# A hybrid decoder step on one core: casts pinned behind evictions, the key and value projection after the query, a norm statistic in another PSUM ring

## The chip, the cores and the metric

The kernel runs on one core of a Trainium2 chip. The metric is the device time of one execution in microseconds. A core has five engines with an in-order queue each: TensorE (PE in the profile, with its weight loads as PEld), VectorE (DVE), ScalarE (ACT), GpSimd (POOL) and SyncE (SP, which here only issues DMAs). ACT and POOL issue DMAs too.

## The reference

```python
h = _rmsnorm(x, n1)
z = h @ w_in
hq, hf, hi, hg, sq, sk, sv, ga, gb = jnp.split(z, np.cumsum(IN_SPLITS)[:-1], axis=-1)
...
m = jax.nn.sigmoid(ga) * y_a + jax.nn.sigmoid(gb) * y_b
x = x + m @ w_o
h2 = _rmsnorm(x, n2)
x = x + jnp.square(jax.nn.relu(h2 @ w_ff1)) @ w_ff2
return x, nk, nv, s_new.astype(x.dtype)
```

One layer, with d_model 1024 and d_ff 4096, is computed for a prompt of 2048 tokens and for 8 sequences of 4 new tokens; `y_a` is a gated recurrence (HGRN2), `y_b` attention over a window of 128 keys with sinks, and a last rmsnorm stands behind the layer. Everything is float32.

## The kernel before

**Precision.** Every float32 operand is kept as two parts in a format that TensorE takes: `hi`, a cast by ACT, and `lo`, the rest, a subtraction on DVE behind it (`split_out` L254 and L255 from a raw tile, `split_in` L148 and L149 in place). A product is then three matmuls, hi·hi, hi·lo and lo·hi (L262 to L264, and L1544 to L1546).

**Stages.** The prompt is worked on in four blocks of 512 tokens; two blocks, with the 32 sample tokens added to the second pair, are one superblock (sb 0 and sb 1). Each large product is done by Strassen's scheme with seven products of half matrices. Three kinds of them matter here:

- `z` (from block 2 on): h @ w_in for all of superblock 1, units `z1_n`. Ahead of it, block 2 projects key and value (`skv`, evicted by `st_skv`, L823) and query (`sq`, `st_sq`, L826) into four tiles `stage` of which each goes out by one DMA to `zqk` (L827, issued by ACT). `late_at(...)` runs, between chunks of these projections, what block 1 has left over: `n2.stat`, `n2.spread` and `h2_out` (L1369, eight POOL stores of the normalised rows `x_b` to `h2d`). The operand `zS3` takes the SBUF slot of `x_b`.
- `f0` and `f1`: the up projection w_ff1 with the squared relu, 16 units per superblock. Unit i does `a` (fB with w1B11, fC with w1B21), `b` (T2, T1, T3) and `c` (T4, B22). The first 6 or 10 units' `a` runs ahead; `Wpair.early` loads and casts their weights. `f1_fin` (L1455 to L1471) forms the sums that the next product needs and POOL stores them in `u_A11` to `u_S4` in DRAM.
- `f2_0` and `f2_1`: the down projection w_ff2 in steps (L1544 to L1546). Step 0 multiplies A12 with the weight block B21. Its groups g = 0 to 3 need an activation tile `f2A12g` (loaded in two halves by `u_load`, L1538) and two weight tiles `rw2B21_<sb><g><h>` (`w2_blk`, L1522); each load is followed by its cast on ACT and its subtraction on DVE. Group 3's second half holds rows that the last unit of f0 (f1) stores (`u_A12_3`).

**Order.** A scheduler lays out the instructions of each engine ahead of time, from its own estimates of when they can run; what is wrapped in `tc.keep_in_program_order` keeps its place in the program on its engine. Tiles come from pools with a fixed number of buffers: the weights from 12 tiles of `wtile`, PSUM from four rings of two banks (`tp`, `hg`, `sw`, `mm`). An instruction that needs a buffer waits in its engine's queue until its last user is done, and what stands behind it there waits too. The statistic of a norm (`stat`, L205) transposes the squares into a bank of a ring (L213, tile `n_fb`) and reduces them on DVE (L214). `n2.ring` names that ring; for the last block it is `hg`, which fC uses too.

## Time and profile before

| | us |
|---|---|
| median of 3 runs | 2850.28 |
| lowest, highest | 2846.7, 2858.54 |
| the profiled execution | 2848.76 |
| its span | 2847.0 |
| PE busy in it | 2744.2 (96%) |
| DVE busy | 1783.7 (63%) |
| ACT busy | 1112.4 (39%) |
| POOL busy | 490.9 (17%) |

The span is the time from the first to the last instruction of the profiled execution; its own time is 1.8 us longer. PE is busy for 96% of it, so what a change to the order can give or take lies in PE's idle time, and that is read from the waits of PE, place by place.

### The profile page before, as it was taken

To read this page: it belongs to the slowest core of one execution; us is meant where nothing else is said; L and a number is where in the kernel's file an instruction comes from. 1 tells how busy PE (TensorE), PEld (TensorE's weight loads), DVE (VectorE), ACT (ScalarE), POOL (GpSimd) and SP (SyncE) were. 2 spreads that over 40 slices of the span, in tenths; PEclk is the share of its full clock that TensorE was granted. 3 is DMA by queue.
4 is the path that set the end of the run, shared out by engine and by line. 5 is a ranking of instruction groups with operands and counts; after the bars stand their busy time and mean duration, and the time that the engine had idled before them with its cause. 6 is when DMAs were issued, how large, how long until landed. Compare 5 with 4: busy or idle time off the path is not lost.

```text
span 2847.0 us, 50088 instructions
## 1 busy us (share of the span) xinstructions
PE 2744.2 (96%) x20053; PEld 2412.9 (85%) x20053; DVE 1783.7 (63%) x2889; ACT 1112.4 (39%) x2070; POOL 490.9 (17%) x782
## 2 busy tenths in 40 slices
PE   8999999999999998999899999999998999999998
PEld 7788887888899967778798888787888999999998
DVE  5675646646765376436666777766567776664546
ACT  4542435323444343324334333424344233343342
POOL 1101211012200102320121122120003333320001
PEclk9999999999999999999999999999999999999999
DMA  5237652377633425541455444686556444485553
GB/s 190 73 113 238 209 180 74 110 244 255 229 127 107 148 88 188 173 136 53 127 171 188 164 159 157 223 307 246 203 182 220 152 148 153 143 292 183 186 188 122
DMA packets 344482, 487.60 MB, mean 171 GB/s; under 512 B 23433, under 2 KB 220825, under 8 KB 344249
## 3 DMA queue, kind: packets, MB, share of 16 engines
q1 hardware_dynamic: 289112, 329.10, 36.6%
q0 software_dynamic: 42880, 140.22, 13.5%
q10 hardware_dynamic: 12256, 15.08, 1.5%
q8 instruction: 157, 2.57, 0.4%
q14 instruction: 77, 0.62, 0.1%
HBM read 353.64 MB, written 130.68 MB: 170 GB/s over the span
## 4 chain that ended last, share of the span: by engine, by line
PE 66%; issue 13%; DMA 7%; DVE 6%; POOL 4%; ACT 3%; POOLq 0%; SPq 0%; ACTq 0%; DVEq 0%
PE f L1544 6%; PE f L1545 6%; PE f L1546 6%; PE fB_f L262 2%; PE fB_f L264 2%; PE fB_f L263 2%; PE fB_z L262 1%; PE fB_z L264 1%; PE fB_z L263 1%; PE wob L1353 1%; PE wob L1354 1%; PE wob L1352 1%; POOL u_S L1471 1%; DMA S<-dS 1%; PE ps_hfb L677 1%
## 5 line engine op out<-in xcount | busy, mean ns | idle before, releaser
L1544 PE MATMUL f<-f2S,hw2T 128*128 128x264 f32 (+1 forms) x576 | 183.9, 319 | 1.8 <-ACT hw2T L148 1.8
L1546 PE MATMUL f<-f2S,lw2T 128*128 128x264 f32 (+1 forms) x576 | 183.7, 319 | 1.6 <-DVE lw2T L149 1.6
L1545 PE MATMUL f<-f2S,hw2T 128*128 128x264 f32 (+1 forms) x576 | 183.5, 319 | 0.0
L262 PE MATMUL fB_f<-S,w1T_f 128*128 128x264 f32 (+1 forms) x384 | 123.1, 321 | 2.5 <-ACT c_f L325 1.7
L1544 PE MATMUL f<-f2A,h_w2B 128*128 128x264 f32 (+1 forms) x384 | 122.4, 319 | 0.0
L1545 PE MATMUL f<-f2A,h_w2B 128*128 128x264 f32 (+1 forms) x384 | 122.3, 319 | 0.0
L1546 PE MATMUL f<-f2A,l_w2B 128*128 128x264 f32 (+1 forms) x384 | 122.3, 318 | 0.0
L263 PE MATMUL fB_f<-S,w1T_f 128*128 128x264 f32 (+1 forms) x384 | 122.3, 319 | 0.0
L264 PE MATMUL fB_f<-S,w1T_f 128*128 128x264 f32 (+1 forms) x384 | 122.1, 320 | 0.0
L149 DVE TENSOR_TENSOR lw2T<-lw2T,hw2T 128x1024 fp32r<-128x1024 f32 x64 | 78.2, 1223 | 66.6 <-ACT hw2T L148 65.7
L148 ACT CAST hw2T<-lw2T 128x1024 fp32r<-128x1024 f32 x64 | 67.2, 1050 | 130.8 <-DMA lw2T<-w_T 130.7
L1352 PE MATMUL wob<-m_b,h_wob 128*128 128x512 f32 (+2 forms) x320 | 114.1, 357 | 3.1 <-ACT m_b L254 3.1
L1544 PEld LDWEIGHTS f<-f2S,hw2T 128*128 128x128 f32 x576 | 108.4, 188 | 10.0 <-ACT hw2T L148 2.7
L1546 PEld LDWEIGHTS f<-f2S,lw2T 128*128 128x128 f32 x576 | 108.0, 188 | 10.0 <-DVE lw2T L149 2.5
L1354 PE MATMUL wob<-m_b,l_wob 128*128 128x512 f32 (+2 forms) x320 | 113.3, 354 | 2.8 <-DVE l_wob L255 2.8
L1353 PE MATMUL wob<-m_b,h_wob 128*128 128x512 f32 (+2 forms) x320 | 113.7, 355 | 1.2 <-DVE m_b L255 1.1
L1545 PEld LDWEIGHTS f<-f2S,hw2T 128*128 128x128 f32 x576 | 108.4, 188 | 7.4
L149 DVE TENSOR_TENSOR f2S<-f2S 128x1024 fp32r<-128x1024 f32 (+1 forms) x64 | 79.0, 1240 | 43.7 <-ACT f2S L148 42.9
L254 ACT CAST w1T_f<-w1r_f 128x512 fp32r<-128x512 f32 x128 | 77.1, 619 | 72.7 <-DVE w1r_f L298 38.4
L255 DVE TENSOR_TENSOR w1T_f<-w1r_f,w1T_f 128x512 fp32r<-128x512 f32 x128 | 87.2, 688 | 26.8 <-ACT w1T_f L254 26.4
L1471 POOL DMA_DIRECT2D u_A<-c_f x106 | 57.3, 541 | 235.8 <-DVE c_f L1455 222.6
L1471 POOL DMA_DIRECT2D u_S<-s_f x144 | 77.7, 540 | 110.9 <-DVE s_f L1466 90.6
(843 smaller groups left out, 9277.2 us busy)
## 6 DMA issues: line engine op xcount, KB each, us to landing
w1r_f<-w_ff SPq DMA_DIRECT2D x64, 512.0 KB
lw2T<-w_T SPq DMA_DIRECT2D x64, 512.0 KB
rw2B<-w_ff SPq DMA_DIRECT2D x48, 512.0 KB
f2S<-u_S SPq DMA_DIRECT2D x32, 528.0 KB
ws<-w_ff SPq DMA_DIRECT2D x32, 512.0 KB
...
```

The source lines that it names most:

```text
L149: nc.vector.tensor_tensor(lo, F(lo), F(hi), ALU.subtract)
L255: nc.vector.tensor_tensor(dl, src, F(dh), ALU.subtract)
L262: nc.tensor.matmul(ps, wh, ah, start=(first and k == 0), stop=False, skip_group_check=not first)
L263: nc.tensor.matmul(ps, wh, al, start=False, stop=False, skip_group_check=not first)
L264: nc.tensor.matmul(ps, wl, ah, start=False, stop=(last and k == 3), skip_group_check=not first)
L1352: nc.tensor.matmul(p, wh, ah, start=(k == 0), stop=False)
L1353: nc.tensor.matmul(p, wh, al, start=False, stop=False)
L1354: nc.tensor.matmul(p, wl, ah, start=False, stop=(k == KD - 1))
L1471: nc.gpsimd.dma_start(us[o][u.n // 4][u.n % 4 * P:(u.n % 4 + 1) * P, u.t0:u.t0 + u.ln], y_)
L1544: nc.tensor.matmul(ps, wh, ah, start=first, stop=False, skip_group_check=cont)
L1545: nc.tensor.matmul(ps, wh, al, start=False, stop=False, skip_group_check=cont)
L1546: nc.tensor.matmul(ps, wl, ah, start=False, stop=lastk, skip_group_check=cont)
```

## The change

It does four things, and no instruction is added or taken away.

1. In block 2 the query is projected first and key and value second. The DMA to `zqk` moves from `st_sq` to `st_skv` with it, and the hooks of `late_at` move: the statistic and the spread run in the query's chunks 0 and 2, `h2_out` in the key and value's.
2. `split_in`, `split_out`, `Wpair.done` and `Wpair.early` get a switch that pins the cast and the subtraction in program order. `strassen_T` sets it for the first pair of each large product (z, f0, f1).
3. `w2_blk` and `u_load` move ahead of the pool of f1's tiles, and a new `begin()` loads and splits group 0 of f2's step 0, pinned; `strassen_T` calls it as `end`, after the last unit's `b` and ahead of its `c`.
4. The last block's `n2.ring` is `sw` and no longer `hg`.

```diff
--- before.py
+++ after.py
@@ -144,9 +144,12 @@
         split_out(wh, wl, raw)
         return wh, wl
 
-    def split_in(hi, lo):
-        nc.scalar.copy(hi, F(lo))
-        nc.vector.tensor_tensor(lo, F(lo), F(hi), ALU.subtract)
+    def pin(x, on=True):
+        return tc.keep_in_program_order(x) if on else x
+
+    def split_in(hi, lo, on=False):
+        pin(nc.scalar.copy(hi, F(lo)), on)
+        pin(nc.vector.tensor_tensor(lo, F(lo), F(hi), ALU.subtract), on)
 
     def unit_rows(w, k0, a, c0, nc_, name):
         src = w[k0 * P:(k0 + a) * P, c0:c0 + nc_].rearrange("(k p) c -> p k c", p=P)
@@ -250,10 +253,9 @@
         def scale(u, k, x):
             nc.vector.scalar_tensor_tensor(x, x, u.w[:, k:k + 1], u.acc, ALU.mult, ALU.mult)
 
-    def split_out(dh, dl, src):
-        nc.scalar.copy(dh, src)
-        nc.vector.tensor_tensor(dl, src, F(dh), ALU.subtract)
-
+    def split_out(dh, dl, src, on=False):
+        pin(nc.scalar.copy(dh, src), on)
+        pin(nc.vector.tensor_tensor(dl, src, F(dh), ALU.subtract), on)
 
     def prod(ps, wv, av, k0, t0, n, first, last=True):
         for k in range(4):
@@ -271,16 +273,16 @@
         def __init__(u, N, n, src, wt):
             u.N, u.n, u.src, u.wt, u.ops = f"{N}_{n}", n, src, wt, {}
 
-        def done(u, name, raw):
+        def done(u, name, raw, on=False):
             v = (u.wt if name in ("T3", "T4") else wtile)(F32R, f"w1{name}_{u.N}").rearrange("p (s k c) -> p s k c", s=2, k=4)
-            split_out(v[:, 0], v[:, 1], raw)
+            split_out(v[:, 0], v[:, 1], raw, on)
             u.ops[name] = v
 
-        def early(u):
+        def early(u, on=False):
             v = wtile(F32, f"w1r0_{u.N}").rearrange("p (s k c) -> p s k c", s=2, k=4)
             for kh in range(2):
                 nc.sync.dma_start(v[:, kh], u.src(u.n, kh)[:, 0:P].rearrange("(k p) c -> p k c", p=P))
-                u.done(f"B{kh + 1}1", v[:, kh])
+                u.done(f"B{kh + 1}1", v[:, kh], on)
 
         def rest(u):
             b = []
@@ -370,7 +372,7 @@
             tt(u.c12, u.pD, u.c12, ALU.add)
             u.fin(u, "c12", u.c12)
 
-    def strassen_T(N, npairs, src, chunks, A, st, fin, ahead, early, mid, free, wt):
+    def strassen_T(N, npairs, src, chunks, A, st, fin, ahead, early, mid, free, wt, end=None):
         ws = [Wpair(N, n, src, wt) for n in range(npairs)]
         nch = len(chunks)
         units = [Unit(i, ws[i // nch], *chunks[i % nch], A, st, fin) for i in range(npairs * nch)]
@@ -378,7 +380,7 @@
             units[-1].free, units[-1].ring = True, mm_ps
         for i in range(ahead):
             if i % nch == 0:
-                units[i].pair.early()
+                units[i].pair.early(i == 0)
             units[i].a(i < 4)
             early(i, units[i])
         for i, u in enumerate(units):
@@ -393,6 +395,8 @@
             u.b()
             if i == 0:
                 mid(u)
+        if end is not None:
+            end()
         units[-1].c()
 
     def chunks_of(n):
@@ -821,13 +825,13 @@
 
             def st_skv(ps, kind, c, nr):
                 nc.scalar.copy(stage[c][:, 512:768], ps)
+                nc.scalar.dma_start(zqk[sb][c * P:(c + 1) * P, :], stage[c])
 
             def st_sq(ps, kind, c, nr):
                 nc.scalar.activation(qk_out(stage[c][:, 0:512]), qk_in(ps), AF.Copy, scale=HD ** -0.5)
-                nc.scalar.dma_start(zqk[sb][c * P:(c + 1) * P, :], stage[c])
-
+
+            colN512(C_SQ, f"sq{B}", st_sq, late_at(0, 2))
             colN(C_SQ + 512, f"skv{B}", st_skv, late_at(1))
-            colN512(C_SQ, f"sq{B}", st_sq, late_at(0, 1))
             Th = Ths[sb]
             r0, r1 = z_half
             A = {"A11": hT_cur[0], "A12": hT_cur[1], "S1": opT(sb, 2, "zS1"), "S2": opT(sb, 3, "zS2"), "S3": opT(sb, 6, "zS3")}
@@ -1369,7 +1373,7 @@
                 nc.gpsimd.dma_start(h2d[sb][k * P:(k + 1) * P, z0:z0 + T], x1[:, k])
 
         if last_b:
-            n2.ring = hg_ps
+            n2.ring = sw_ps
         late += [n2.stat, n2.spread] + ([] if last_b else [h2_out])
     wk_ctx.close()
     cm_ctx.close()
@@ -1419,6 +1423,47 @@
         KG = NP // 4
         OPS = ("A11", "A12", "A22", "S1", "S2", "S3", "S4")
         us = {o: [tc.dram_tile([4 * P, Th], F32, name=f"u_{o}_{g}_{sb}") for g in range(KG)] for o in OPS}
+
+        slots = iter([0, 1] + [2, 3, 4, 5] * 8)
+        def w2_blk(o, k0, nk, c0, nc_, name, on=False):
+            r0, cs = k0 * P, slice(c0, c0 + nc_)
+
...
+            N = f"w2{o}_{name}"
+            if o[0] == "T":
+                wh, wl = wtile(F32R, "h" + N), wtile(F32R, "l" + N)
+                load(o, F(wl))
+                split_in(wh, wl, on)
+                return v3(wh), v3(wl)
+            x = wtile(F32, "r" + N)
+            load(o, x)
+            wh, wl = wtile(F32R, "h_" + N), wtile(F32R, "l_" + N)
+            split_out(wh, wl, x, on)
+            return v3(wh), v3(wl)
+
+        def u_load(o, g, on=False):
+            av = opv(next(slots), f"f2{o}{g}")
+            for k in range(0, 4, 2):
+                nc.sync.dma_start(lo_(av)[:, k:k + 2], us[o][g][k * P:(k + 2) * P, :].rearrange("(k p) t -> p k t", p=P))
+                split_in(av[:, 0, k:k + 2], av[:, 1, k:k + 2], on)
+            return av
+
+        begun = {}
+
+        def begin():
+            ao, wo = steps[0]
+            begun[ao] = u_load(ao, 0, True)
+            begun[wo] = [w2_blk(wo, 2 * h, 2, 0, 512, f"{sb}0{h}", True) for h in range(2)]
 
         with tc.tile_pool(name=f"f1_{sb}", bufs=1, reuse_waits="tile") as fp:
             def get(nm, slot):
@@ -1473,7 +1518,7 @@
             strassen_T(f"f{sb}", NP, lambda n, kh: w1[kh * 4 * P:(kh + 1) * 4 * P, 2 * n * P:2 * (n + 1) * P],
                        chunks, ff_ops,
                        lambda ln, name: fp.tile([P, ln], F32, tag="st", bufs=12 * len(chunks), name=name),
-                       f1_fin, 6 if len(chunks) == 1 else 10, early, mid, True, lambda dt, name: fp.tile([P, 1024], dt, tag="we", bufs=2, name=name))
+                       f1_fin, 6 if len(chunks) == 1 else 10, early, mid, True, lambda dt, name: fp.tile([P, 1024], dt, tag="we", bufs=2, name=name), begin)
 
         last = sb == nsb - 1
         fresh = (True, True, False, True, True, False, True)
@@ -1485,7 +1530,6 @@
         else:
             rings = ((tp_ps, hg_ps, mm_ps, sw_ps),) * 6 + ((hg_ps, mm_ps, sw_ps, hg_ps),)
         last = sb == nsb - 1
-        slots = iter([0, 1] + [2, 3, 4, 5] * 8)
         with tc.tile_pool(name=f"f2_{sb}", bufs=1, reuse_waits="tile") as fp:
             if last:
                 y1, xo = None, raw8(6, Th, f"xo{sb}")
@@ -1506,38 +1550,6 @@
                     return xo[:, regs[r], t0:t0 + ln]
 
                 return Fin(off[sb] + o * Th + t0, ln, lambda j: yacc[o][j][:, t0:t0 + ln], x, f2_ns, q)
-
-            def w2_blk(o, k0, nk, c0, nc_, name):
...
-            def u_load(o, g):
...
 
             def gemm2(ps, wh, wl, av, t0, ln, k, first, lastk, cont=False):
                 ah, al = av[:, 0, k, t0:t0 + ln], av[:, 1, k, t0:t0 + ln]
@@ -1571,8 +1583,9 @@
                     todo = [lambda: f0.sq(4, 5), lambda: f0.sq(6, 7), none, f0.stat, none, none, f0.spread] + [lambda j=j: f0.out(j) for j in range(KD)]
                     late_ops = []
                 for g in range(KG):
-                    av = u_load(ao, g)
-                    wb = [w2_blk(wo, 4 * g + 2 * h, 2, 0, 512, f"{sb}{g}{h}") for h in range(2)]
+                    first = si == 0 and g == 0
+                    av = begun[ao] if first else u_load(ao, g)
+                    wb = begun[wo] if first else [w2_blk(wo, 4 * g + 2 * h, 2, 0, 512, f"{sb}{g}{h}") for h in range(2)]
                     for j in range(4):
                         js = slice(j * P, (j + 1) * P)
                         for k in range(4):
```

Three places of the order follow, first of before, then of now.

SP where f0 ends and f2_0 begins. `rw2B21_0gh` is half h of group g's weights, `f2A12g` and `f2S1g` are activation tiles, `xo` are rows that superblock 1 needs later.

Before:

```order
L1522 DMA rw2B21_000_17497<-w_ff2 128x2x512
L1522 DMA rw2B21_001_17503<-w_ff2 128x2x512
L1538 DMA f2A120_0_17490<-u_A12_0_0_15048 128x2x512 x2
L1538 DMA f2A121_0_17561<-u_A12_1_0_15049 128x2x512 x2
L1522 DMA rw2B21_010_17568<-w_ff2 128x2x512
L1538 DMA f2S10_0_17772<-u_S1_0_0_15056 128x2x512 x2
L1538 DMA f2S11_0_17864<-u_S1_1_0_15057 128x2x512
L1522 DMA rw2B21_011_17574<-w_ff2 128x2x512
L1538 DMA f2A122_0_17628<-u_A12_2_0_15050 128x2x512 x2
L1538 DMA f2A123_0_17695<-u_A12_3_0_15051 128x2x512
L1522 DMA rw2B21_020_17635<-w_ff2 128x2x512
L1538 DMA f2S11_0_17864<-u_S1_1_0_15057 128x2x512
```

Now:

```order
L1440 DMA rw2B21_000_17435<-w_ff2 128x2x512
L1457 DMA f2A120_0_17428<-u_A12_0_0_15048 128x2x512 x2
L1457 DMA f2A121_0_17561<-u_A12_1_0_15049 128x2x512 x2
L1457 DMA f2S10_0_17772<-u_S1_0_0_15056 128x2x512 x2
L1457 DMA f2S11_0_17864<-u_S1_1_0_15057 128x2x512 x2
L1457 DMA f2A122_0_17628<-u_A12_2_0_15050 128x2x512 x2
L1457 DMA f2A123_0_17695<-u_A12_3_0_15051 128x2x512
L1440 DMA rw2B21_001_17441<-w_ff2 128x2x512
L1440 DMA rw2B21_010_17568<-w_ff2 128x2x512
L1457 DMA f2A123_0_17695<-u_A12_3_0_15051 128x2x512
L1440 DMA rw2B21_011_17574<-w_ff2 128x2x512
L591 DMA xo0_17496<-h2d1_103 128x512
```

The load of `rw2B21_001` stood second and stands behind the first half of `f2A123`; that of `rw2B21_011` stood ahead of both halves of `f2A123` and stands behind both.

SP where f1 ends and f2_1 begins, with the same names.

Before:

```order
L1522 DMA rw2B21_100_23926<-w_ff2 128x2x512
L1522 DMA rw2B21_101_23932<-w_ff2 128x2x512
L1522 DMA rw2B21_110_24045<-w_ff2 128x2x512
L1522 DMA rw2B21_111_24051<-w_ff2 128x2x512
L1538 DMA f2A120_1_23919<-u_A12_0_1_19571 128x2x528 x2
L1538 DMA f2A121_1_24038<-u_A12_1_1_19572 128x2x528 x2
L1522 DMA rw2B21_120_24160<-w_ff2 128x2x512
L1538 DMA f2S10_1_24399<-u_S1_0_1_19579 128x2x528
L1538 DMA f2A122_1_24153<-u_A12_2_1_19573 128x2x528 x2
L1538 DMA f2A123_1_24268<-u_A12_3_1_19574 128x2x528
L1538 DMA f2S10_1_24399<-u_S1_0_1_19579 128x2x528
L1538 DMA f2S11_1_24516<-u_S1_1_1_19580 128x2x528
```

Now:

```order
L1440 DMA rw2B21_100_23853<-w_ff2 128x2x512
L1457 DMA f2A120_1_23846<-u_A12_0_1_19571 128x2x528 x2
L1457 DMA f2A121_1_24038<-u_A12_1_1_19572 128x2x528 x2
L1457 DMA f2S10_1_24399<-u_S1_0_1_19579 128x2x528 x2
L1457 DMA f2A122_1_24153<-u_A12_2_1_19573 128x2x528 x2
L1457 DMA f2A123_1_24268<-u_A12_3_1_19574 128x2x528
L1440 DMA rw2B21_101_23859<-w_ff2 128x2x512
L1457 DMA f2S11_1_24516<-u_S1_1_1_19580 128x2x528 x2
L1457 DMA f2A123_1_24268<-u_A12_3_1_19574 128x2x528
L1440 DMA rw2B21_110_24045<-w_ff2 128x2x512
L1440 DMA rw2B21_111_24051<-w_ff2 128x2x512
```

Four weight loads stood ahead of every activation load; now one does, and `rw2B21_110` and `rw2B21_111` stand behind the second half of `f2A123`.

ACT where f0 begins. `nq_fb3` are squares of the last norm, `w1B11_f0_n` and `w1B21_f0_n` the casts of the weights of unit n.

Before:

```order
L241 ACTIVATE nq_fb3_14770<-x1_b3_14515 128x544
L254 CAST h_wob361_14926<-r_wob361_14924 128x1024
L241 ACTIVATE nq_fb3_14783<-x1_b3_14515 128x544
L254 CAST w1B11_f0_0_15077<-w1r0_f0_0_15075 128x512
L254 CAST w1B21_f0_0_15081<-w1r0_f0_0_15075 128x512
L254 CAST w1B11_f0_1_15125<-w1r0_f0_1_15123 128x512
L241 ACTIVATE nq_fb3_14908<-x1_b3_14515 128x544
L254 CAST w1B21_f0_1_15129<-w1r0_f0_1_15123 128x512
L241 ACTIVATE nq_fb3_14914<-x1_b3_14515 128x544
L254 CAST w1B11_f0_2_15178<-w1r0_f0_2_15176 128x512
```

Now:

```order
L244 ACTIVATE nq_fb3_14770<-x1_b3_14515 128x544
L257 CAST h_wob361_14926<-r_wob361_14924 128x1024
L244 ACTIVATE nq_fb3_14783<-x1_b3_14515 128x544
L244 ACTIVATE nq_fb3_14908<-x1_b3_14515 128x544
L244 ACTIVATE nq_fb3_14914<-x1_b3_14515 128x544
L244 ACTIVATE nq_fb3_15032<-x1_b3_14515 128x544
L244 ACTIVATE nq_fb3_15038<-x1_b3_14515 128x544
L257 CAST w1B11_f0_0_15077<-w1r0_f0_0_15075 128x512
L257 CAST w1B21_f0_0_15081<-w1r0_f0_0_15075 128x512
L151 CAST S3_0_15114<-S3_0_15114 128x1024 x2
```

The casts of the first units' weights stood between the squares and stand behind the last of them.

## Rows read from the trace of the kernel before

**Rows 1.** Section 1 of the page, the whole execution: busy time, share of the span and instructions of each engine.

```profile
...
PE 2744.2 (96%) x20053; PEld 2412.9 (85%) x20053; DVE 1783.7 (63%) x2889; ACT 1112.4 (39%) x2070; POOL 490.9 (17%) x782
...
```

**Rows 2.** The view of PE's waits, one answer for each of five stretches in the order 720 to 800, 1520 to 1570, 1835 to 1860, 1905 to 1930 and 2480 to 2520 us. Columns: what waited, what it waited for, then us in total, times, and the longest in us.

```profile
...
PE fB_z L262 <- ACT stg L826: 2.3, 1, 2.3
PE fC_z L262 <- DVE p_z L340: 2.2, 1, 2.2
PE ps_skvb L174 <- DVE l_skvb L255: 0.6, 1, 0.6
...
PE n_fb L213 <- DVE p_f L340: 5.3, 1, 5.3
...
PE fD_f L262 <- DVE c_f L357: 2.3, 1, 2.3
...
PE f L1544 <- ACT hw2T L148: 1.8, 2, 1.6
PE f L1546 <- DVE lw2T L149: 1.6, 2, 1.1
...
PE fB_f L262 <- ACT c_f L325: 1.4, 1, 1.4
```

**Rows 3.** The table by stretches. Columns: stretch, its length, busy us and instructions of PE, PEld, DVE, ACT and POOL, the granted TensorE clock as a share of full speed, the DMA engines' share, GB/s.

```profile
...
1545.00:1553.00 8.00, 6.06 (x18) 4.83 (x19) 6.68 (x10) 2.79 (x5) 3.53 (x2) 0.57 0.12 44
1835.00:1850.00 15.00, 12.67 (x57) 10.15 (x56) 12.33 (x16) 9.09 (x10) 2.74 (x6) 1.00 1.00 367
1850.00:1870.00 20.00, 20.00 (x90) 16.58 (x89) 10.71 (x12) 5.01 (x6) 9.46 (x18) 1.00 1.00 368
2505.00:2530.00 25.00, 25.00 (x209) 25.00 (x209) 16.83 (x19) 12.43 (x13) 11.20 (x21) 1.00 1.02 381
...
```

**Rows 4.** The timeline of ACT from 722 to 792 us (z projection). Columns: start in us, duration in us, engine, line, operation, out<-in, shapes, count, and in brackets the idle time before it and what ended it.

```profile
...
759.44 2.23 ACT L254 CAST zS<-zh 128x528 fp32r<-128x528 f32 x4
...
764.74 0.33 ACTq L827 DMA_DIRECT2D zqk<-stg  x1
...
774.09 0.94 ACT L325 COPY p_z<-fB_z 128x264 f32<-128x264 f32 x3 [7.55 <-DMA zqk<-stg]
...
```

**Rows 5.** The timeline of POOL at the same place, and the row on landing that the view of line L1369 gives for 700 to 800 us.

```profile
...
752.52 0.54 POOL L1369 DMA_DIRECT2D h2d<-x_b  x1 [1.56 <-DMA zS<-zS]
...
DMA to landing us min/median/max: 5.7/6.5/7.2
```

**Rows 6.** The timeline of PE there: the first matmul of the z product.

```profile
...
762.22 0.39 PE L262 MATMUL fB_z<-hT,w1B_z 128*128 128x264 f32 x1 [2.30 <-ACT stg L826]
...
```

**Rows 7.** The timeline of ACT where the first large product f0 begins.

```profile
...
1529.27 0.66 ACT L241 ACTIVATE nq_fb<-x_b 128x544 f32<-128x544 f32 x1 [1.44 <-DVE x_b L1358]
1530.32 0.62 ACT L254 CAST w1B_f<-w1r_f 128x512 fp32r<-128x512 f32 x1 [0.39 <-DMA w1r_f<-w_ff]
...
```

**Rows 8.** The timeline of PE there: the first matmul of f0.

```profile
...
1528.56 0.40 PE L262 MATMUL fB_f<-A,w1B_f 128*128 128x512 f32 x1
...
```

**Rows 9.** The timeline of SP (its queue of DMAs) from 1815 to 1890 us, where f0 ends and f2_0 begins.

```profile
...
1841.37 0.46 SPq L1522 DMA_DIRECT2D rw2B<-w_ff  x1
...
1856.63 0.36 SPq L1538 DMA_DIRECT2D f2A<-u_A  x1
...
1859.66 0.52 SPq L1522 DMA_DIRECT2D rw2B<-w_ff  x1
...
1863.98 0.38 SPq L1522 DMA_DIRECT2D rw2B<-w_ff  x1
...
1877.23 0.33 SPq L587 DMA_DIRECT2D xo<-h2d  x1
...
```

**Rows 10.** The timeline of POOL there.

```profile
...
1848.29 2.13 POOL L1590 DMA_DIRECT2D y<-x1d  x4
1850.41 0.54 POOL L1471 DMA_DIRECT2D u_A<-c_f  x1
...
```

**Rows 11.** The timeline of ACT there.

```profile
...
1849.13 1.04 ACT L254 CAST h_w2B<-rw2B 128x1024 fp32r<-128x1024 f32 x1
...
1863.94 1.05 ACT L148 CAST f2A<-f2A 128x1024 fp32r<-128x1024 f32 x1 [9.76 <-DMA f2A<-u_A]
1867.44 1.05 ACT L254 CAST h_w2B<-rw2B 128x1024 fp32r<-128x1024 f32 x1 [2.44 <-DMA rw2B<-w_ff]
...
1875.52 1.05 ACT L254 CAST h_w2B<-rw2B 128x1024 fp32r<-128x1024 f32 x1 [5.81 <-DMA rw2B<-w_ff]
...
```

**Rows 12.** The timeline of PE there: the first matmul of f2_0.

```profile
...
1846.12 0.39 PE L1544 MATMUL f<-f2A,h_w2B 128*128 128x512 f32 x1
...
```

**Rows 13.** The timeline of SP from 2465 to 2535 us, where f1 ends and f2_1 begins.

```profile
...
2502.47 1.82 SPq L1538 DMA_DIRECT2D f2A<-u_A  x3
...
2516.68 0.36 SPq L1538 DMA_DIRECT2D f2A<-u_A  x1
2517.09 0.46 SPq L1538 DMA_DIRECT2D f2S<-u_S  x1
...
```

**Rows 14.** The timeline of ACT there.

```profile
...
2513.50 1.08 ACT L148 CAST f2S<-f2S 128x1056 fp32r<-128x1056 f32 x1 [0.22 <-DMA f2S<-u_S]
...
2522.24 1.08 ACT L148 CAST f2S<-f2S 128x1056 fp32r<-128x1056 f32 x1 [0.27 <-DMA f2S<-u_S]
...
```

**Rows 15.** The timeline of PE there: the first matmul of f2_1.

```profile
...
2503.74 0.28 PE L1544 MATMUL f<-f2A,h_w2B 128*128 128x264 f32 x1
...
```

34 lines of the change are left out of this document (9 added, 25 removed).

## The prediction

> **What bounds the kernel now.** Read the page's busy times first: PE is busy 2744.2 of 2847.0 us [rows 1], so the core is bound by TensorE, no work is added or taken away, and the change can only open or close PE's idle stretches, 102.8 us in all. Read next which of them lie where the change moves something: PE's own waits in five stretches [rows 2]. At the start of z it waits 2.3 us for the evictions of the query, 2.2 us for a row of the first units' sums and 0.6 us for a weight part. At the start of f0 it waits 5.3 us, once, for a bank of the `hg` ring. At the end of f0 it waits 2.3 us in `c`, some 60 us into f2_0 1.8 and 1.6 us for weights, and at the end of f1 1.4 us. That is 17.5 us. Last, read the granted clock by stretches [rows 3]: it is 0.57 from 1545 to 1553 us, right behind the wait of 5.3, and 1.00 around the wait of 2.3 at the end of f0. PE's 6.06 busy us there, at 0.57 of the full clock, are worth 3.5 at the full one, so about 2.6 are lost to the lower of the two levels, 1.2 GHz. All waits and the clock together, 20.1 us, are the most that the change can give, and 0.5% of the time, about what a measurement of this kernel can tell from no change, is 14.3 us.
>
> The same table shows what the new order leans on: from 1835 to 1870 and from 2505 to 2530 the DMA engines' share is 1.00 to 1.02 at 367 to 381 GB/s. Whatever is loaded there is paced by the memory traffic, not by its issue.
>
> **Query first, key and value behind (z).** ACT writes the query out after its last chunk; PE's wait of 2.3 us is for that, since the first product's bank is one of the query's. With the query in front, that wait goes. Behind it stands another: the cast of `zS3` cannot start until the eight stores of `x_b` to `h2d` have landed; the last leaves at 752.52 and they take 5.7 to 7.2 us to land [rows 5], so the cast starts near 759.4, as it does now [rows 4]. In the new order of ACT the eviction of the second key and value chunk stands behind that cast (0.56 us, a quarter of 2.23) and takes about 0.4 us: a bank is free at about 760.3. The fourth chunk, 24 matmuls of 0.12 us, needs it, and ends at about 763.1. The z product starts there, 0.9 us later than 762.22 [rows 6]. The wait of 2.2 us came from ACT's copies that waited for the `zqk` stores, the last issued at 764.74 and landed by 774.09 [rows 4]; now two leave before 761.5 and the last at about 763.5, with less of a pile, so most of this wait goes, and the 0.6 us on the key and value's weight part goes because its parts are made long ahead. Sum: 0.9 − 2.2 − 0.6 = **−1.9 us**. Bounds: if the stores land earlier, all three waits go, −5.1; if the `zqk` stores still take 9.3 us and the second wait only shrinks, +0.5, and with a lost clock behind a longer wait, +2.
>
> **Statistic in `sw`, casts of unit 0 pinned (f0).** The transposes of the statistic take a `sw` bank, so they no longer wait for fC's eviction: −5.3 us, and the clock that falls behind it −2.6. Against it, the pinned casts of unit 0 stand behind the last square of the norm, which starts at 1529.27 and takes 0.66 us; the first cast then ends near 1530.5, and the first matmul, which starts at 1528.56 right behind the output projection, moves to about 1530.5: +1.9 [rows 7, 8]. The next casts stand behind two casts of an operand on ACT, about 1 us each; I take +1.5 for them (0 to 3). Sum: −5.3 − 2.6 + 1.9 + 1.5 = **−4.5 us**, between −7.9 (nothing new waits) and −1 (the wait behind the last square is 4 us and the clock falls there).
>
> **Begin ahead of the last `c` (f0 to f2_0).** The wait of 2.3 in `c` stays, to about 0.3: DVE still splits `f2S10` ahead of the two sums on which `c` waits. What changes is SP. A load on SP's queue that waits holds back all behind it. The second half of `f2A123` waits until the last unit's store has landed; before it is issued at 1856.63 [rows 9], the store having left POOL at 1850.41 [rows 10], 6.2 us earlier. Ahead of it, `rw2B21_011` had long left, at 1841.37 [rows 9], and was cast at 1849.13 [rows 11]. Now this load stands behind it. On POOL all eight loads of `y`, 0.53 us each, come ahead of more of the stores (seven ahead of this one instead of the four at 1848.29); the store leaves at about 1852, lands at about 1858.2, and `rw2B21_011` leaves at about 1858.7. A load of 512 KB here takes 7.3 us (1856.63 to 1863.94) or 7.8 (1859.66 to 1867.44) to its cast [rows 9, 11]: I take the first, so its cast begins at 1866 and ends at 1867.1. PE reaches it after 66 matmuls of 0.22 us (20.0 us for 90) [rows 3] from 1846.12 [rows 12], at about 1861 and with the small waits ahead of it 1861.9. **New wait 5.2 us.** Its low part comes 1.3 us after that. Smaller ones: the subtractions of the first weight and of `f2A120` now stand behind the last unit's sums on DVE, +0.5; `rw2B21_001` and `010`, +0.5; the low parts of `020` and `021`, +1.6. `030` and `031` left at 1859.66 and 1863.98, ahead of the `xo` load at 1877.23 [rows 9] that waits for POOL's stores; now they stand behind it, so `030` lands at about 1884.5 and is cast by 1885.5, while PE, pushed back by the waits so far, is there 144 matmuls from the start (32 us) at about 1885; `031` follows 4 us later: +0.8, +3.9 and +0.5. Later waits of 1.8 and 1.6 vanish, since the product starts late and its weights do not, −3.4, and 0.3 goes in `c`. Sum: 5.2 + 1.3 + 0.5 + 0.5 + 1.6 + 5.2 − 3.4 − 0.3 = **+10.6 us**. Bounds: a load of 5.2 us, the fastest row of this kind (2517.09 to 2522.24) [rows 13, 14], takes 2.1 from the first wait and about as much from the last: +5; a load of 11.5 us (1863.98 to 1875.52) [rows 9, 11] makes it +17.
>
> The Trainium skill prices such a transfer otherwise: its page "DMA: Bandwidth & Descriptors", section "Anatomy of one DMA — SWDGE (gpsimd) path", fits 2.0 us and the bytes at 436 GB/s, which by that page would be an estimate of 3.2 us for 512 KB; the rows above show 7.3 and 7.8, since the DMA share is 1.00 there, so the trace disagrees for this stretch. By the page's figure the first wait would be 1.1 us and the sum +3.
>
> **Begin, the second time (f1 to f2_1).** Before, four weight loads were issued from 2471.60 to about 2492, ahead of all; now `rw2B21_101` stands behind the first half of `f2A123`, so it leaves where the next load did, at about 2504.3 (2502.47 and 1.82) [rows 13], and lands as that one did, for a cast at 2513.50 less the 0.3 us that ACT was behind [rows 14]: cast by 2513.3 to 2514.5. PE starts f2_1 at 2503.74 [rows 15] and needs it after 60 instructions of 0.12 us (25.0 us for 209) [rows 3], at 2511: +2.2. `rw2B21_110` now stands behind the second half of `f2A123`, which waits to 2516.68 [rows 13] for a store; it leaves at 2517.0, lands at 2522.2 as the load of 2517.09 does, and is cast by 2523.3. PE is there 108 instructions from the start, at 2516.7 and 2.2: +4.4. If the end of f1 comes 1.4 us sooner, all of this shifts with it. Low parts, +1.4; the wait of 1.4 goes, −1.4. Sum: 2.2 + 4.4 + 1.4 − 1.4 = **+6.6 us**, between +3 (loads 2 us faster) and +10.
>
> **The clock.** A wait of about 5 us is what the clock fell behind at f0 [rows 2, 3]; two of the new waits are near that. Much of what PE then loses lies beside loads that it would wait for anyway, so I take +1.7 for both, between 0 and 6.
>
> **Sum:** −1.9 − 4.5 + 10.6 + 6.6 + 1.7 = +12.5 us on the profiled execution's 2848.76, that is 2861.3; the same on the median of 2850.28 is 2862.8. I take 2862, 0.4% above the median.
>
> **Rivals.**
>
> *Slower by more than 0.5%.* The mechanism is the queue of SP at the two starts of f2: a weight load behind an activation load that waits for the last unit's store. It decides the sign of the measurement from the point where these loads take 8 us or more to their cast, or where the clock falls behind each of three waits. For it speak the DMA share of 1.00 and the row of 11.5 us; against it the rows of 7.3 and 5.2. Price: f2_0 +15, f2_1 +8, the clock +4, less 6.4 at z and f0: +20.6, about 2871.
>
> *The order helps as it says.* If `begin` brings the first casts early and SP never stands, all removed waits are kept: 5.1 + 7.9 + 2.3 + 3.4 + 1.4 = 20.1 less, 2830. For it speaks that the first activation loads no longer stand behind the second weight's; against it that only group 0 is moved ahead, that group 1's and even group 0's second weight stand behind `f2A123` in the new order, and that a store has to land first.
>
> *The new waits at f2 are half of mine*, because the loads run faster once fewer are in flight: f2_0 +4, f2_1 +3, no clock: 7.0 − 6.4, 2850.9.
>
> *The pinning does nothing.* The order shown speaks against it: the casts of unit 0 stand behind the last square, and SP's order is another. Its time would be 2850; it lies in the case above.
>
> **How the numbers follow.** My forecast 0.44 (2854 to 2864), slower 0.40 (2864.5 to 2878), half the waits or nothing done 0.10 (2846 to 2854), the order helps 0.06. Faster 0.06, within 0.5% 0.54, slower 0.40. The range leaves out the case that helps and a part of the slow one: 2846 to 2876.
>
> **What the profile after would show.** Right: a wait of 4 to 6 us in f2_0 for the cast of group 1's second weight, one of 3 to 5 us in f2_1, the wait of 5.3 on `n_fb` gone with its low clock, a wait of about 2 us ahead of f0's first matmul, and the z product starting at 762.5 to 764 us. Wrong: `rw2B21_011` issued before 1850, its cast before 1860, or the transposes of `n_fb` still waiting.

## The result and the profile after

| | before | after |
|---|---|---|
| median of 20 runs, us | 2855.6 | 2862.65 |
| lowest, highest | 2846.7, 2865.03 | 2854.62, 2867.77 |
| profiled execution's span | 2847.0 | 2856.1 |
| PE busy in it | 2744.2 | 2745.0 |

The ratio is 1.002, with a 95% interval of 1.0011 to 1.0029: slower by 3 to 8 us, less than the 0.5% within which the text called it no change. The median of before over these 20 runs lies 5 us above the one of the three runs shown ahead of the prediction; the time that was predicted, 2862, is met, but the step that was predicted, +12, is twice what the ratio shows. That the time itself came out within 1 us is luck: a step twice too large was added to a median that was 5 us too low.

PE's work is the same, so the two traces are compared by the start of each stage on PE, its first matmul, and by PE's waits. The first matmuls of z, f0, f2_0 and f2_1 stood at 762.22, 1528.56, 1846.12 and 2503.74 us [rows 6, 8, 12, 15]. In the trace of after, in PE's timeline at those four places:

```profile
...
762.98 0.42 PE L264 MATMUL fB_z<-hT,w1B_z 128*128 128x264 f32 x1
...
1525.32 0.50 PE L264 MATMUL fB_f<-A,w1B_f 128*128 128x512 f32 x1 [1.77 <-ACT w1B_f L257]
...
1834.74 0.39 PE L1556 MATMUL f<-f2A,h_w2B 128*128 128x512 f32 x1
...
2498.98 0.53 PE L1556 MATMUL f<-f2A,h_w2B 128*128 128x264 f32 x3
```

| stretch | before | after | difference |
|---|---|---|---|
| start to the first matmul of z | 762.2 | 763.0 | +0.8 |
| z to the first matmul of f0 | 766.3 | 762.3 | −4.0 |
| f0 to the first matmul of f2_0 | 317.6 | 309.4 | −8.1 |
| f2_0 and f1, to the first of f2_1 | 657.6 | 664.2 | +6.6 |
| f2_1 to the end of the span | 343.3 | 357.1 | +13.9 |

So 11.4 us were won by the start of f2_0 and 20.5 lost after it. The fourth row holds two things: cut at the first matmul of f1 (2159.46 us before, 2156.90 after), f2_0 takes 8.9 us more and f1 2.2 less. PE's waits at the same places as in [rows 2], in the stretches 720 to 800, 1515 to 1575, 1835 to 1870, 1870 to 1940 and 2480 to 2540 us of after (columns as there):

```profile
...
PE ps_skvb L176 <- ACT stg L827: 1.8, 1, 1.8
...
PE fB_f L264 <- ACT w1B_f L257: 1.8, 1, 1.8
PE fB_f L266 <- DVE w1B_f L258: 0.6, 1, 0.6
...
PE f L1556 <- ACT h_w2B L257: 4.2, 1, 4.2
PE f L1558 <- DVE l_w2B L258: 1.5, 2, 1.2
...
PE f L1556 <- ACT h_w2B L257: 2.1, 1, 2.1
PE f L1556 <- ACT hw2T L151: 1.3, 1, 1.3
PE f L1558 <- DVE lw2T L152: 0.5, 1, 0.5
PE f L1558 <- DVE l_w2B L258: 0.4, 1, 0.4
...
PE f L1556 <- ACT h_w2B L257: 7.2, 2, 6.4
PE f L1558 <- DVE l_w2B L258: 1.1, 1, 1.1
```

Read it against [rows 2]. In z three waits of 5.1 us became one of 1.8. The wait of 5.3 on `n_fb` is gone, and 1.8 and 0.6 us for the pinned casts stand in its place. In f2_0 there are new waits of 4.2 and 2.1 us for casts of weights, in f2_1 one of 6.4. What is ahead of each such cast shows in SP's and ACT's timelines. SP in the trace of after where f0 ends and f2_0 begins, then ACT there (the places of [rows 9] and [rows 11]):

```profile
...
1831.61 0.97 SPq L1440 DMA_DIRECT2D rw2B<-w_ff  x2
1846.72 0.37 SPq L1457 DMA_DIRECT2D f2A<-u_A  x1
1847.13 0.51 SPq L1440 DMA_DIRECT2D rw2B<-w_ff  x1
...
```

```profile
...
1852.19 1.04 ACT L151 CAST f2A<-f2A 128x1024 fp32r<-128x1024 f32 x1 [10.96 <-DMA f2A<-u_A]
1853.53 1.04 ACT L257 CAST h_w2B<-rw2B 128x1024 fp32r<-128x1024 f32 x1 [0.29 <-DMA rw2B<-w_ff]
...
```

Before, on SP and on ACT, the load of group 1's second weight and its cast:

```profile
...
1835.97 0.52 SPq L1522 DMA_DIRECT2D rw2B<-w_ff  x1
...
1843.65 1.05 ACT L254 CAST h_w2B<-rw2B 128x1024 fp32r<-128x1024 f32 x1 [0.24 <-DMA rw2B<-w_ff]
...
```

By the order of SP's list this load is `rw2B21_011`; the load of 1841.37 in [rows 9], with its cast at 1849.13 in [rows 11], is the next weight of that list, `rw2B21_020`. After, `rw2B21_011` left at 1847.13, right behind the second half of `f2A123` at 1846.72 and 15 us behind the two weights ahead of it. Before, it had left 10 us ahead of f2_0's first matmul; now it leaves 12 us behind it. Its cast stands at 1853.53 on ACT, behind the cast of that half, for which ACT had waited 10.96 us. At f2_1 the same happens to group 1's first weight, `rw2B21_110`: PE waits 6.38 us for the cast that SP's load of 2512.94 feeds, issued behind the half of `f2A123` at 2512.48; on ACT that cast (2521.01) stands behind the half's (2517.39).

```profile
...
2512.48 0.36 SPq L1457 DMA_DIRECT2D f2A<-u_A  x1
2512.94 10.76 SPq L1440 DMA_DIRECT2D rw2B<-w_ff  x5
```

```profile
...
2517.39 1.07 ACT L151 CAST f2A<-f2A 128x1056 fp32r<-128x1056 f32 x1 [2.50 <-DMA f2A<-u_A]
2521.01 1.04 ACT L257 CAST h_w2B<-rw2B 128x1024 fp32r<-128x1024 f32 x1 [2.55 <-DMA rw2B<-w_ff]
...
```

The table by stretches for after (columns as in [rows 3]) shows the clock: full from f0's first matmul to 35 us behind it, where before it was 0.57 from 16 to 24 us behind it, and below full behind each of the new long waits.

```profile
...
1523.00:1545.00 22.00, 19.55 (x90) 15.41 (x89) 17.84 (x26) 14.54 (x22) 8.21 (x10) 1.00 0.95 299
1545.00:1560.00 15.00, 15.00 (x73) 12.22 (x72) 13.86 (x23) 6.27 (x13) 3.28 (x4) 1.00 0.59 188
1850.00:1870.00 20.00, 14.64 (x56) 10.70 (x55) 11.86 (x16) 5.46 (x6) 6.95 (x13) 0.91 0.87 309
1870.00:1890.00 20.00, 17.50 (x70) 13.74 (x69) 11.38 (x17) 5.36 (x6) 3.24 (x6) 0.91 0.87 293
2520.00:2530.00 10.00, 7.90 (x42) 7.90 (x43) 5.01 (x5) 3.15 (x3) 2.24 (x5) 0.59 1.04 389
...
```

### The profile page after: what moved, and what is told of

The parts are those of the page before. It is cut to its first block, busy times and chain, and to the rows that moved or that the text cites. A ratio compares the mean times of both kernels' runs of the same rounds, so it can differ in the third digit from the quotient of the medians.

```text
span 2856.1 us, 50050 instructions
## 1 busy us (share of the span) xinstructions
PE 2745.0 (96%) x20053; PEld 2411.8 (84%) x20053; DVE 1782.6 (62%) x2889; ACT 1110.9 (39%) x2070; POOL 495.5 (17%) x782
## 4 chain that ended last, share of the span: by engine, by line
PE 66%; issue 12%; DMA 8%; DVE 6%; POOL 3%; ACT 3%; SPq 0%; POOLq 0%; DVEq 0%; ACTq 0%
PE f L1556 6%; PE f L1557 6%; PE f L1558 6%; PE fB_f L264 2%; PE fB_f L266 2%; PE fB_f L265 2%; PE fB_z L264 1%; PE fB_z L266 1%; PE fB_z L265 1%; PE wob L1358 1%; PE wob L1357 1%; POOL u_S L1516 1%; PE wob L1356 1%; DMA S<-dS 1%; PE gab L167 1%
## 5 line engine op out<-in xcount | busy, mean ns | idle before, releaser
L151 ACT CAST f2S<-f2S 128x1024 fp32r<-128x1024 f32 (+1 forms) x64 | 68.1, 1065 | 87.6 <-DMA f2S<-u_S 83.2
```

The lines of the kernel that those rows point to most:

```text
L151: pin(nc.scalar.copy(hi, F(lo)), on)
```

## Experiments

Each kernel was timed in turn with the kernel before; ratios are to that, with 95% intervals. `e1` to `e4` take the change apart, `e7` and `e8` take f0's part apart, and the others ask why `begin()` costs. The edits of `e3`, `e4`, `e7` and `e8` are shown against the kernel before, the others against the whole change; `...` stands for what is left out. [rows 2] has the columns of PE's waits.

**e1, everything but begin().**

```diff
-  ..., lambda dt, name: fp.tile(...), begin)
+  ..., lambda dt, name: fp.tile(...))
-                    first = si == 0 and g == 0
+                    first = False
```

> All of the change except begin(): group 0 of f2's step 0 is loaded and split where it was before. My theory, that all of the loss comes from begin() and the rest gains: the z product starts about 0.8 us later, the 2.2 us wait in z and the 5.3 us wait on n_fb with its low clock stay gone, and no wait over 2 us stands in f2_0 or f2_1; 5 to 12 us faster than before (ratio 0.996 to 0.998). Rival, that f2 waits because everything in front of it came sooner and its loads did not: waits of 4 to 6 us stay at both starts of f2 and the time is within 3 us of before or above it.

Measured: 0.995 (0.9935 to 0.9965), 2843.0 us at the median against 2856.0. The gain is 10 to 19 us, and no wait for a cast of a weight stands at the starts of f2. PE's waits from 1515 to 1575, 1825 to 1890 and 2480 to 2540 us:

```profile
...
PE fB_f L264 <- ACT w1B_f L257: 1.8, 1, 1.8
...
PE fD_f L264 <- DVE c_f L359: 1.2, 1, 1.2
...
PE fB_f L264 <- ACT c_f L327: 1.9, 1, 1.9
...
```

A wait of 2.4 us for a cast of the next step's weights stands 84 us into f2_0, where before had one of 1.6. The rival, that f2 must wait because all in front of it came sooner, falls. This is the fastest of the kernels by ratio.

**e2, begin() alone** on the kernel before (the swap, the ring and `early(i == 0)` undone).

```diff
-                units[i].pair.early(i == 0)
+                units[i].pair.early()
-            n2.ring = sw_ps
+            n2.ring = hg_ps
...
```

> The kernel before with begin() alone. My theory: waits of about 4 us and 2 us in f2_0 and of about 6 us in f2_1 for casts of weights, 12 to 20 us slower than before (ratio 1.004 to 1.007). Rival, that begin() costs only because f0 and z came sooner: within 4 us of before.

Measured: 1.0049 (1.0033 to 1.0065), 9 to 19 us slower. f2_0 waits 4.5 and 3.9 us and f2_1 6.0 us for casts of weights, as in the whole change (PE's waits from 1825 to 1890, 1890 to 1940 and 2480 to 2540 us):

```profile
...
PE f L1556 <- ACT h_w2B L257: 4.5, 1, 4.5
...
PE f L1556 <- ACT h_w2B L257: 3.9, 1, 3.9
...
PE f L1556 <- ACT h_w2B L257: 6.8, 2, 6.0
...
```

`begin()` costs this whether or not the stages in front came sooner.

**e3, the ring and the pins at the starts, without the swap and without begin().**

```diff
-            n2.ring = hg_ps
+            n2.ring = sw_ps
-                units[i].pair.early()
+                units[i].pair.early(i == 0)
```

> The kernel before with the statistic in the sw ring and the pinned casts of the first pair of each large product, without the swap of query and key and value and without begin(). My theory: the wait of 5.3 us on n_fb and the stretch at 0.57 of the clock are gone, waits of 1.8 and 0.6 us stand ahead of f0's first matmuls; 4 to 6 us faster than before (ratio about 0.998). Rival, that the wait on n_fb only hid later waits for casts: within 2 us of before.

Measured: 0.9967 (0.9953 to 0.9981), 5 to 13 us faster; the stretch from f0's first matmul to f2_0's is 310.3 us in its trace, against 317.6. Its waits of 1.8 and 0.6 us at f0 are those of the whole change.

**e4, the swap of query and key and value alone.**

```diff
+                nc.scalar.dma_start(zqk[sb][c * P:(c + 1) * P, :], stage[c])   # in st_skv, no longer in st_sq
+            colN512(C_SQ, f"sq{B}", st_sq, late_at(0, 2))
             colN(C_SQ + 512, f"skv{B}", st_skv, late_at(1))
-            colN512(C_SQ, f"sq{B}", st_sq, late_at(0, 1))
```

> The kernel before with the query ahead of key and value alone. My theory: one wait of about 1.8 us for a bank in the key and value projection in place of waits of 2.3, 2.2 and 0.6 us, the z product starts within 1 us of where it did, 1 to 4 us faster than before. Rival, from the two traces, where 5.8 us were gone between z's first and f0's first matmul: 5 to 7 us faster.

Measured: 0.9998 (0.9986 to 1.0009), no change that can be told. PE's waits in z, 720 to 800 us:

```profile
...
PE ps_skvb L176 <- ACT stg L827: 1.7, 1, 1.7
PE fC_z L264 <- DVE c_z L342: 1.6, 1, 1.6
PE fC_z L264 <- DVE p_z L342: 0.9, 1, 0.9
```

The three waits of 5.1 us became a bank's wait of 1.7 and two on the sums of the first units, 1.6 and 0.9. What went came back a few matmuls on. The z product started at 764.30, 2.1 us later than before and not within 1 us as expected; a wait of 1.7 us at 720 us lies ahead of it. The −4.0 between z and f0 in the two traces is not the swap's: e5, e9 and e10, which have the same code from z to f0, show 770.1, 755.8 and 764.7 us for that stretch, so one trace tells nothing there under some 14 us.

**e5, the late load in another queue.** The half of `f2A123` that waits for a store is issued by POOL, so SP's weights don't stand behind it.

```diff
-                nc.sync.dma_start(lo_(av)[:, k:k + 2], us[o][g]...
+                (nc.gpsimd if o == "A12" and g == KG - 1 and k else nc.sync).dma_start(lo_(av)[:, k:k + 2], us[o][g]...
```

> The whole change, but the one load of f2's step 0 that waits for the last unit's store (second half of f2A123) is issued by POOL, not SP, so that no weight load stands behind it. My theory, that SP's queue is what makes the casts of group 1's second weight late: the waits of 4.2 us in f2_0 and 6.4 us in f2_1 fall below 2 us each, and the time is 8 to 16 us under that of the whole change. Rival, that the weights are late because the DMA engines are full there: waits of 3 us and more stay, and the time is within 4 us of the whole change.

Measured: 1.0015 (1.0005 to 1.0025), hardly under the whole change, and the waits stayed: 4.4 us in f2_0 and 6.4 in f2_1 (PE's waits from 1825 to 1890 and 2480 to 2550 us).

```profile
...
PE f L1556 <- ACT h_w2B L257: 4.4, 1, 4.4
...
PE f L1556 <- ACT h_w2B L257: 7.0, 2, 6.4
...
```

My theory falls in the form that I gave it. The rival's numbers came true, but not its reason, as SP's and ACT's timelines at f2_0 show:

```profile
...
1843.29 1.49 SPq L1440 DMA_DIRECT2D rw2B<-w_ff  x3
...
```

```profile
...
1864.86 1.04 ACT L151 CAST f2A<-f2A 128x1024 fp32r<-128x1024 f32 x1 [12.29 <-DMA f2A<-u_A]
1865.81 1.04 ACT L257 CAST h_w2B<-rw2B 128x1024 fp32r<-128x1024 f32 x1
...
```

Three weights left in a row from 1843.29, before f2_0's first matmul at 1846.52, so group 1's second weight was no longer late in leaving. Its cast at 1865.81 has no wait of its own: it follows the cast of the late half at 1864.86, for which ACT had idled 12.29 us. This suggests that the wait is held twice, by SP's order and by ACT's; e9 and e10 ask it.

**e6, weights ahead of activations inside begin().**

```diff
-            begun[ao] = u_load(ao, 0, True)
             begun[wo] = [w2_blk(wo, 2 * h, 2, 0, 512, f"{sb}0{h}", True) for h in range(2)]
+            begun[ao] = u_load(ao, 0, True)
```

> The whole change with the two weight blocks ahead of the activation loads inside begin(). Only the second block of group 0 moves up on SP, by one load; group 1's second block still stands behind the load that waits for a store. My theory: the waits of about 4 and 6 us stay, within 4 us of the whole change. Rival, that group 0's own weight sets the loss: 6 us and more under the whole change.

Measured: 1.0005 (0.9994 to 1.0015), 4 us under the whole change, which lies between what the two theories gave; the intervals overlap. The waits changed their name and place: 4.5 us in f2_0 and 8.0 in f2_1, now ahead of the first matmul and for casts of activations. In f2_1 the cast that ends the wait (2505.48 on ACT) follows the one of group 0's second weight (2504.53), which the pinned order now puts ahead of it and whose load left SP only at 2495.76. Inconclusive on the weight's share.

**e7, the ring alone, and e8, the pins of the first pairs alone.**

```diff
-            n2.ring = hg_ps
+            n2.ring = sw_ps
```

> The kernel before with the statistic of the last norm in the sw ring alone. My theory: the wait of 5.3 us on n_fb and the low clock behind it go, and f0 starts without a wait, so 6 to 9 us faster than before. Rival, that without the pinned casts the n_fb transposes or f0's next matmuls wait for casts instead: under 3 us faster.

```diff
-                units[i].pair.early()
+                units[i].pair.early(i == 0)
```

> The kernel before with the pinned casts of the first pair of each large product alone, the statistic still in the hg ring. My theory: the wait of 1.8 us ahead of f0 and 0.6 us in it come on top, and the wait on n_fb stays or shrinks a little; 0 to 4 us slower than before. Rival, that the pinning itself brings the gain: 4 us and more faster.

Measured: e7 1.0 (0.999 to 1.0011), e8 0.9985 (0.9973 to 0.9997). PE's waits from 1515 to 1575 us, e7 first and then e8:

```profile
...
PE fB_f L264 <- ACT carry L229: 3.7, 1, 3.7
...
PE fB_f L264 <- ACT w1B_f L257: 1.8, 1, 1.8
PE fB_f L266 <- DVE w1B_f L258: 0.6, 1, 0.6
PE n_fb L216 <- DVE p_f L342: 0.6, 1, 0.6
```

Both theories fall and both rivals hold. The ring alone moves the wait: the 5.3 us on `n_fb` are gone, and a first product of a later unit, whose bank is of the `sw` ring as well, waits 3.7 us for the norm's spread to be copied out. The pins alone nearly remove the wait on `n_fb` (0.6 of 5.3), at the price of 1.8 and 0.6 us. Both together gave 0.9967 (e3) and the parts sum to 0.9985, but the intervals of e3 and e8 overlap. From f0's first matmul to f2_0's the traces give the whole gain to the pins: 310.1 us in e8 and 310.3 in e3, against 317.6 before and 315.5 in e7. What e8 lacks lies behind that, from f2_0's first matmul to f1's (318.3 us against 314.0 in e3); why is not shown.

**e9, ACT's order changed: the casts of all four groups of step 0 pinned.**

```diff
-                    av = begun[ao] if first else u_load(ao, g)
+                    av = begun[ao] if first else u_load(ao, g, si == 0)
-                    wb = begun[wo] if first else [w2_blk(..., f"{sb}{g}{h}") for h in range(2)]
+                    wb = begun[wo] if first else [w2_blk(..., f"{sb}{g}{h}", si == 0) for h in range(2)]
```

**e10, that and the load of e5.**

> The whole change, and the casts and subtractions of all four groups of f2's step 0 are pinned too, so that on ACT and DVE the casts of group 1's second weight stand ahead of those of the second half of f2A123; on SP its load still stands behind that half's load. New theory after the runs so far, that the late store holds the weight back twice, by SP's order and by ACT's, and either alone suffices: the waits of about 4 us in f2_0 and 5 to 6 us in f2_1 stay, within 4 us of the whole change. Rival, that ACT's order alone makes the wait: waits fall below 2 us and the time is 6 us and more under the whole change.

> The same, and the second half of f2A123 is loaded by POOL, so that the weight stands ahead of it on SP, on ACT and on DVE. New theory: the wait for group 1's second weight goes at both starts of f2 (below 1.5 us each), 8 us and more under the whole change and under before by 0 to 8 us. Rival, that the DMA engines are full there whatever the order: waits of 3 us and more stay and the time is within 4 us of the whole change.

Measured: e9 1.0008 (1.0 to 1.0017), e10 0.9996 (0.9985 to 1.0008). In f2_0 e9 is the counterpart of e5. The load of group 1's second weight still left SP behind the late half (1845.48 us), its cast on ACT no longer stood behind that half's, and PE still waited 3.3 us for it. On SP, ACT and PE:

```profile
...
1845.89 0.50 SPq L1440 DMA_DIRECT2D rw2B<-w_ff  x1
...
1852.11 1.04 ACT L257 CAST h_w2B<-rw2B 128x1024 fp32r<-128x1024 f32 x1 [11.24 <-DMA rw2B<-w_ff]
...
1853.21 0.80 PE L1556 MATMUL f<-f2A,h_w2B 128*128 128x512 f32 x1 [3.29 <-ACT h_w2B L257]
...
```

PE's waits in f2_1 in e10, 2480 to 2550 us, and then in f2_0, 1825 to 1900:

```profile
...
PE f L1556 <- ACT h_w2B L257: 3.2, 2, 2.3
...
PE f L1556 <- ACT h_w2B L257: 7.2, 2, 4.2
...
```

In f2_1 the wait of 6.4 us, for group 1's first weight, fell to 0.9 (in e9 to 1.5; there the new pins brought the weight's load ahead of the late half on SP too, which I had not expected). The 2.3 that is the largest left in e10 is for group 0's second weight. In f2_0 the wait for group 1's weight went in e10 and another of 4.2 us stood one group on, for a weight whose load was issued at 1861.76, behind an `xo` load that SP could issue only at 1860.36:

```profile
...
1860.36 0.34 SPq L591 DMA_DIRECT2D xo<-h2d  x1
...
1861.76 0.38 SPq L1440 DMA_DIRECT2D rw2B<-w_ff  x1
...
```

Against the whole change e10 wins 0.24%, some 7 us; in the traces the stretch from f2_1 to the end of PE's work shows 9 (349.6 to 340.4 us), and that of f2_0, 322.1 us against 322.2, nothing. The theory of two orders holds for the waits that it named; in f2_0 another wait of the same size takes the place, behind another load.

**e11, begin() not pinned.**

```diff
-            begun[ao] = u_load(ao, 0, True)
-            begun[wo] = [w2_blk(wo, 2 * h, 2, 0, 512, f"{sb}0{h}", True) for h in range(2)]
+            begun[ao] = u_load(ao, 0)
+            begun[wo] = [w2_blk(wo, 2 * h, 2, 0, 512, f"{sb}0{h}") for h in range(2)]
```

> The whole change, but what begin() loads and splits is not pinned; group 0's code stands ahead of the last c all the same. SP's order at both starts of f2 is then that of the kernel before. My theory, that the pinning and not the place in the code makes the loss: within 4 us of the run without begin(), about 10 us under before (ratio 0.994 to 0.998). Rival, that the place makes it: slower than before.

Measured: 0.9965 (0.9953 to 0.9978). The code stands where the change put it and SP's order at both starts is that of before: the loss is the pins', not the place's. Its interval overlaps with that of e1. It answers the rival of full DMA engines too: from f2_0's first matmul on, 1843.9 to 1873.9 us, their share was 1.00 at 364 GB/s, as much as in the whole change (0.98 at 352), and PE did not wait once in these 30 us.

**e12, as e10, and the `xo` rows loaded by POOL.**

```diff
-                nc.sync.dma_start(x[:, 0:cut], h2d[b][rows, c0:c0 + cut])
+                nc.gpsimd.dma_start(x[:, 0:cut], h2d[b][rows, c0:c0 + cut])
...
```

> As the run with both orders changed, and the rows xo of superblock 1 are loaded by POOL and not SP, so that group 2's weights in f2_0 stand behind no load that waits. Theory, that what is left in f2_0 (4.2 and 3.1 us) is the same thing one group on, weights behind the xo loads on SP: the loads of group 2's weights leave 10 us sooner against the end of f0, both waits fall below 1.5 us, and the time is 4 to 9 us under that run (ratio to before 0.996 to 0.998). Rival, that these weights are late for the traffic itself: the waits stay within 1.5 us of what they were and so does the time within 3 us.

Measured: 0.9972 (0.9959 to 0.9985), 4 to 12 us under before, as the theory had it, but not for its reason. On PE, 1825 to 1900 us, and on DVE there:

```profile
...
PE f L1558 <- DVE l_w2B L258: 8.8, 1, 8.8
```

```profile
...
1852.29 0.24 DVE L595 SCALAR_TENSOR_TENSOR xo<-xo,cols,carry 128x16 f32<-128x16 f32 x1 [13.91 <-DMA xo<-x1d]
1852.44 1.22 DVE L258 TENSOR_TENSOR l_w2B<-rw2B,h_w2B 128x1024 fp32r<-128x1024 f32 x1
...
```

The weights' loads left early, in one row of seven from 1818.8, and the wait went to a third queue: the subtraction of the weight (1852.44) stands on DVE behind a row operation on `xo` (1852.29) that idled 13.91 us for its load. f2_0 did not get shorter (327 us to f1's first matmul, against 322 in e10). In the traces what was won lies ahead of f0, which began at 1512.2 us against 1531.1 in e10; the same function loads rows for superblock 0 there. It was not taken apart, and a stretch there can differ by 14 us from trace to trace.

**All runs side by side.** Three stretches in us, from first matmul to first matmul, the last one to the end of PE's work:

| kernels | f0 to f2_0 | f2_0 to f1 | f2_1 to the end |
|---|---|---|---|
| no pins at all: before, e4, e7 | 315.5 to 317.6 | 313.3 to 314.8 | 335.6 to 337.7 |
| first casts pinned, `begin()` absent or not pinned: e1, e3, e8, e11 | 310.1 to 310.4 | 314.0 to 318.3 | 335.8 to 337.3 |
| `begin()` pinned, first casts not: e2 | 315.0 | 323.9 | 348.5 |
| the whole change, e5 | 309.4, 310.0 | 322.2, 322.1 | 349.6, 350.4 |
| the same with changed orders: e9, e10, e12 | 309.4 to 310.2 | 322.1 to 327.5 | 339.5 to 341.0 |
| weights first: e6 | 314.0 | 312.7 | 337.4 |

In e6 the waits stand ahead of f2_0 and f2_1, so they count in the stretch in front: 314.0, and 350.6 from f1 to f2_1 where the others show 341 to 346. Apart from e6, the pins of the first casts shorten f0 in every kernel that has them, and a pinned `begin()` lengthens f2_0 and f2_1 in every kernel that has it. The changed orders gave back most of the loss in f2_1 and none of it in f2_0.

## Why the prediction was right, and where it was off

**The bound, right.** PE's busy time moved by 0.8 us, all the rest is waits and the clock.

**Two readings.** The prediction says that `rw2B21_011` left at 1841.37 and was cast at 1849.13 before; by SP's list these are the times of `rw2B21_020`, and `rw2B21_011` left at 1835.97 and was cast at 1843.65. The sum does not use them. Two of the signs by which it was to be known as wrong came true as they are written, `rw2B21_011` issued before 1850 (1847.13) and cast before 1860 (1853.53), but only because f2_0 began 11.4 us sooner: counted from f2_0's first matmul the load was issued at 12.4 us, where 12.6 was worked out.

**z, −1.9: right in kind.** The trace shows the wait for a bank in the key and value projection, 1.8 us, and the product's start at 762.98, +0.8 where +0.9 was worked out. Alone the swap gives −0.6 us (−4 to +3), which can't be told from nothing: e4 shows two waits on the first units' sums that the sum had taken as gone.

**f0, −4.5: right in sign, its reason wrong in part.** With the pins and the ring it measured −5 to −13 (e3). The +1.9 ahead of the first matmul was 1.77 in the trace, the +1.5 for the next casts 0.6, and the clock stayed full. But I gave the whole −5.3 to the ring and booked the pins as a cost alone. The step that failed is "The transposes of the statistic take a `sw` bank, so they no longer wait for fC's eviction": alone that wins nothing that can be told (e7), because it puts the bank's next user behind the norm's spread, a wait of 3.7 us. The pins alone take the wait on `n_fb` from 5.3 to 0.6 us (e8), and f0 is as short with them alone (310.1 us) as with both (310.3).

**begin() at f2_0, +10.6: right in kind, too large.** A wait of 5.2 us was worked out for the cast of group 1's second weight, and 4.16 measured; the next of 3.9 measured 2.1. The new waits add up to 8.2 us, where 14.3 had been priced, and of the later waits of 3.4 that were to vanish 1.8 stayed. From f2_0's first matmul to f1's the trace shows +8.9, but some 3 of that are the clock's. The late half was issued 12.0 us behind f2_0's first matmul, as worked out, but the weight's cast began 6.4 us after its issue (1847.13 to 1853.53), not 7.3. The Trainium skill, page "DMA: Bandwidth & Descriptors", section "Anatomy of one DMA — SWDGE (gpsimd) path", gives its fit for transfers that GpSimd issues; the estimate of 3.2 us from it was for a load that SP issues, and this row does not agree with it either.

**begin() at f2_1, +6.6: the waits right in sum, not one by one.** From f2_1 to the end +13.9 us were measured. The three waits priced there at 4.4, 2.2 and 1.4 us measured 6.38, 0.77 and 1.1, so 8.2 in all against 8.0, but only because errors cancel: the largest lies outside the 3 to 5 us that the prediction named, since its load took 8.1 us to its cast (2512.94 to 2521.01) and not 5.2. The rest of the 13.9 is the clock and smaller waits.

**The clock, +1.7: the term that was mis-sized.** In f2_1 PE's 7.90 busy us from 2520 to 2530 at 0.59 lose 3.2, and in f2_0 its 14.64 and 17.50 busy us at 0.91 lose 2.9: some 6 us in all, an estimate from these rows. I had assumed that most of it would lie beside loads that PE waits for anyway.

**Which rival.** The slower rival's mechanism, weights behind a load that waits for the last unit's store, is the one that acts, at less than the price given there. The sentence that SP's queue is what holds them was half of it. For the wait on group 1's second weight in f2_0, undoing SP's order alone left 4.4 us (e5) and undoing ACT's alone 3.3 (e9); with both undone that wait went (e10). At f2_1 ACT's order alone was not tested, since e9 moved the load on SP as well. e12 shows DVE as a third place. That the pinning makes the loss, and not the earlier place, is shown (e1, e2, e11). That the waits account for all of f2_0's part is not: no order with `begin()` pinned brought f2_0 and what stands ahead of it back. Why the scheduler puts the second and later weights behind once the first casts are pinned stays open: the buffers do not force it, since e11 has the same loads in the order of before, and the scheduler's estimates are not in a trace.

**The sum.** +12.5 was worked out; the two traces differ by 9.1, the runs by 3 to 8. The parts measured alone, +14.0 (e2), −9.4 (e3) and −0.6 (e4), add up to +4.0, which the interval of the whole holds. Against the sum, f0 won twice what was given to it and `begin()` cost less, 14.0 against 17.2 and the clock, so the sum was too high from both sides, and the predicted time was met because the median of three runs of before lay low.
